# A Hymba layer on one core: the per-layer-embedding projection moved, operands and splits respread, two gate products reordered

## The chip, the cores and the metric

The kernel runs on one core of a Trainium2 chip. The metric is the device time of one execution in microseconds (us), taken as the median of several runs. Beside it stands one profiled execution, from which all rows below come.

## The reference, cut to what matters

One decoder layer for 512 positions of width 2048, in float32. The change touches what stands behind the mixers:

```
h = h + concat([oa, ob, oc]) @ w_out                  # 2048 x 2048
c = rmsnorm(h, ffn_norm)
hg = causal_conv3(c @ w_gate) + conv_b                # 2048 x 5632
h = h + (gelu(hg) * (c @ w_up)) @ w_down              # 5632 x 2048
e = rmsnorm(h, ple_norm)
h = h + sigmoid(e @ w_ple_gate) * (p @ w_ple_proj)    # 2048 x 2048 and 256 x 2048
```

## The kernel before, in words

**Split products.** Each float32 operand is split in two float32r parts, high and low, and a product is three matmuls: high x high, high x low, low x high. A weight chunk is split by a cast on ScalarE (L163, tile `wh`) and a subtraction on VectorE (L164, `wl`).

**Stages on TensorE, in order of time:** the input projection and the mixers, to about 785 us; `w_out`, four column blocks, the last one in two halves, to about 900; `w_gate` and `w_up` as Strassen-Winograd products of 2x2 blocks (classes Pair and Product, seven products P1 to P7 a pair) to about 1793; `w_down` in three passes over 44 row tiles, the first for column blocks 0 and 1 in eight PSUM banks, the second for block 2 and the third for block 3 in four; `w_ple_gate` as Winograd products by halves (classes Columns and Half, `run_half` L450, column blocks c = 0 to 3) from about 2314 to 2488; then the tail of the last output tiles. The projection of p by `w_ple_proj`, 16 banks of six matmuls, is spliced into the second pass of `w_down`; its results go to DRAM (`ppd`) and come back as `pp` when a gate block is finished (`finish_ple`, L521).

**What sets the order.** Everything is issued in program order, and each engine takes its instructions in that order. Side work is written as Python generators in the list `bg`; `tick()` (L129), called at fixed places between matmul groups, takes one step of each. So a `yield` more in a generator moves all that follows it by one tick. `later` holds evictions that are issued after the next product or half. `advance_split(upto)` (L341) issues the two split instructions of the weight chunks up to a number, and whatever combination of blocks on VectorE they need (L251, L254, L306 to L312); the number says how far ahead of their use chunks are split. DMAs are issued on SyncE's queue (SP), in program order too; one that writes a buffer still in use holds up those behind it.

**Buffers.** 69 pages of 128x512 float32 (`page`, L94) serve nearly everything: residual tiles `h`, normalised sums, `hid`, `ppe`, `ps`, `pu`. Of weight chunks there are 4 high and 4 low buffers and 3 raw ones. PSUM has 4 `g` and 4 `m` banks; `x` of a gate block is a `g` bank, `y` and `z` are `m` banks.

**Steps that the change touches.** `operands` (L1245): transposes of h on TensorE (L1264) into an `m` bank, copies to SBUF on ScalarE with the norm's gain (L1266), then sums on VectorE (L1282) and splits (ScalarE L1294, VectorE L1299). `evac_o2` (L1209) adds a `w_out` bank to the residual (L1212), `evac_down` (L1455) a `w_down` bank (L1458). `stat` (L647) sums squares on ScalarE (L649), `finish` (L651) makes 1/rms of them on GpSimd (L118 to L122), `broadcast` (L658) spreads it over the partitions by matmuls (L667). `hid_split` (L1409) loads a tile of the hidden layer and splits it (L1415, L1417). `load_p` (L1481) loads p and transposes it (L1492). `evac_half` (L485) copies `x` to SBUF (L488) and adds halves (L495).

Of the kernel before, what the change touches and what calls it, by code (L numbers as in the profile page):

```python
# [52 lines left out]
def hybrid_layer_kernel(  # L53
# [343 lines left out]
    def run_product(c, ks):  # L397
# [3 lines left out]
        advance_split(products[0, "P1"].i + 4 if ks[-1] < 7 else c.i + 3)  # L401
# [48 lines left out]
    def run_half(c):  # L450
# [17 lines left out]
        for k in range(4):  # L468
            ah, al = eop[OPERAND[kind], 4 * h + k]
            for t in range(2):  # L470
                o, a = ps[:, t * 256 : t * 256 + 256], slice(t * P, t * P + P)
                f = st and h == 0 and k == 0 and t == 0
                skip = t == 1 or not st
                PE.matmul(o, ah[:, a], vh[:, k, :], start=f, stop=False, skip_group_check=skip)  # L474
                PE.matmul(o, ah[:, a], vl[:, k, :], start=False, stop=False, skip_group_check=skip)
                PE.matmul(o, al[:, a], vh[:, k, :], start=False, stop=h == 1 and k == 3, skip_group_check=skip)
            if k == 1:
                tick()
        while later:
            later.pop(0)()  # L480
# [4 lines left out]
    def evac_half(g, kind):  # L485
        if kind in ("P1", "P6", "P7"):
            g.s[kind] = page("ps")
            ACT.copy(g.s[kind], g.x)  # L488
        if kind in ("P2", "P7", "P3"):
            q, a, th, s = dict(P2=(g.__dict__.get("y"), "P1", 0, 0), P7=(g.z, "P7", 1, 1), P3=(g.z, "P6", 0, 1))[kind]  # L490
            u = page("pu")
            if kind == "P3" and g.c == 3:
                for i in range(2):
                    v = slice(i * 256, i * 256 + 256)
                    DVE.tensor_tensor(u[:, v], q[:, v], g.s[a][:, v], op=ALU.add)  # L495
                    for _ in finish_ple(g, u, th, s, u, [i]):
                        pass
                return
# [9 lines left out]
    def run_groups(on_start=None):  # L508
# [20 lines left out]
        splice(flat)  # L529
# [87 lines left out]
    class Act:  # L617
# [615 lines left out]
    def stats_store(c):  # L1233
        while state["operands"] < 2 * c + 1:
            yield
        for t in range(NT):
# [3 lines left out]
            yield  # L1240
        if c == 3:
# [3 lines left out]
    def operands(kps, gain, dst):  # L1245

        m, n = T // 2, len(kps)
        if n > 1 and dst is eop and kps[0] == 6:
            at = [[page("at").rearrange("p (i t) -> p i t", i=2) for _ in range(2)] for _ in range(2)]
        else:  # L1250
            if n > 1:
                at = [xtile("T").rearrange("p (i t) -> p i t", i=2) for _ in range(2)]
            elif kps[0] == 6:
                t = xtile("T").rearrange("p (r i t) -> p r i t", r=2, i=1)
                at = [t[:, r, :, :] for r in range(2)]
            else:
                at = [page("at").rearrange("p (i t) -> p i t", i=1) for _ in range(2)]
            at = [[t[:, :, :m], t[:, :, m:]] for t in at]
        for k in range(2 * n):
# [11 lines left out]
        (a11, a21), (a12, a22) = at  # L1271

        while n == 1 and kps[0] == 6 and "mixed" not in state:
            yield
        temps = []
        if n == 1 and kps[0] == 6:
# [25 lines left out]

        p1 = high("A11", a11)
        s1 = temp(a21, a22, ALU.add)
        p5 = high("S1", s1)
        low(*p1)
        s2 = temp(s1, a11, ALU.subtract)
        p2 = high("A12", a12)
        low(*p5)
        low(*p2)  # L1310
# [462 lines left out]
```

## Time and profile before

| | us |
|---|---|
| median of 3 runs | 2497.28 (2496.26 to 2498.15) |
| profiled execution | 2497.11 |
| its span, first to last instruction | 2495.4 |
| TensorE busy in the span | 2464.0 |
| VectorE busy | 1534.4 |
| ScalarE busy | 1065.4 |

TensorE is busy nearly all the time, so the interest lies in the stretches where it is not, and in those where its clock fell from 2.4 to 1.2 GHz. A view by windows gives for each stretch the busy time of each engine, the share of full clock that was granted, and the DMA share; the view of waits names who ended TensorE's idle times; the timeline of an engine then shows what stood in its queue.

### The profile page before, as it was taken

How to read it: one execution, taken by the hardware profiler on the slowest of the kernel's cores; microseconds unless marked ns; L12 is line 12 of the kernel's file. 1: busy time of each engine (PE TensorE's matmuls, PEld its weight loads, DVE VectorE, ACT ScalarE, POOL GpSimd, SP SyncE). 2: the span in 40 equal slices, each digit the busy share in tenths (PEclk: the TensorE clock that was granted, in tenths of full speed). 3: DMA queues.
4: the chain of work that ended last, by engine and by line, in shares of the span. 5: the costliest groups of instructions: out<-in, count | busy, mean ns of one | idle time of the engine just before them, and what ended most of it. 6: DMA issues, size and time to landing. Idle time of an engine off the chain costs nothing.

```text
span 2495.4 us, 38383 instructions
## 1 busy us (share of the span) xinstructions
PE 2464.0 (99%) x15628; PEld 2225.0 (89%) x15628; DVE 1534.4 (61%) x2021; ACT 1065.4 (43%) x1612; POOL 140.1 (6%) x232
## 2 busy tenths in 40 slices
PE   9999999999999999999999999999999999999898
PEld 7888898888888889999999999999988877878898
DVE  5253535545465578888878888888633355354787
ACT  5222234444442454444444444444432254253544
POOL 1232400201000000000000000000000000000100
PEclk9999999999999999999999999999999999999999
DMA  5322222233233333434434343434444457666455
GB/s 178 102 68 85 69 85 81 81 93 93 84 108 113 119 120 110 127 115 122 120 110 128 110 129 108 127 115 123 148 142 145 143 189 238 198 222 205 126 186 186
DMA packets 324635, 321.45 MB, mean 129 GB/s; under 512 B 13691, under 2 KB 243812, under 8 KB 324458
## 3 DMA queue, kind: packets, MB, share of 16 engines
q1 hardware_dynamic: 324426, 319.00, 42.0%
q8 instruction: 122, 2.00, 0.3%
q14 instruction: 55, 0.45, 0.1%
q10 hardware_dynamic: 32, 0.01, 0.0%
HBM read 290.63 MB, written 28.32 MB: 128 GB/s over the span
## 4 chain that ended last, share of the span: by engine, by line
PE 95%; DVE 2%; DMA 1%; ACT 1%; issue 0%; POOL 0%; SPq 0%; ACTq 0%; DVEq 0%
PE g L388 13%; PE g L386 13%; PE g L387 13%; PE x L420 7%; PE x L418 7%; PE x L419 7%; PE m L420 5%; PE m L418 5%; PE m L419 5%; PE m L388 2%; PE m L387 2%; PE m L386 2%; PE g L379 1%; PE g L381 1%; PE g L380 1%; PE x L474 1%
## 5 line engine op out<-in xcount | busy, mean ns | idle before, releaser
L164 DVE TENSOR_TENSOR wl<-raw,wh 128x1024 fp32r<-128x1024 f32 (+1 forms) x334 | 411.2, 1232 | 403.2 <-ACT wh L163 401.9
L163 ACT CAST wh<-raw 128x1024 fp32r<-128x1024 f32 (+1 forms) x334 | 347.0, 1042 | 339.3 <-PE g L388 250.7
L418 PE MATMUL x<-sh,wh 128*128 128x256 f32 x1408 | 397.5, 282 | 0.1
L420 PE MATMUL x<-sh,wl 128*128 128x256 f32 x1408 | 397.3, 282 | 0.0
L419 PE MATMUL x<-sl,wh 128*128 128x256 f32 x1408 | 396.9, 282 | 0.0
L164 DVE TENSOR_TENSOR wl<-T,wh 128x1024 fp32r<-128x1024 f32 x208 | 254.4, 1223 | 133.9 <-ACT wh L163 132.8
L420 PE MATMUL m<-sh,wl 128*128 128x256 f32 x1056 | 298.7, 283 | 0.0
L418 PE MATMUL m<-sh,wh 128*128 128x256 f32 x1056 | 298.7, 283 | 0.0
L419 PE MATMUL m<-sl,wh 128*128 128x256 f32 x1056 | 298.4, 283 | 0.0
L386 PE MATMUL g<-wh,ah 128*128 128x512 f32 (+2 forms) x768 | 297.0, 387 | 1.2 <-ACT ah L641 1.2
L388 PE MATMUL g<-wh,al 128*128 128x512 f32 (+2 forms) x768 | 289.2, 377 | 0.0
L387 PE MATMUL g<-wl,ah 128*128 128x512 f32 (+2 forms) x768 | 288.0, 375 | 0.0
L418 PEld LDWEIGHTS x<-sh,wh 128*128 128x128 f32 x1408 | 267.5, 190 | 0.3 <-ACT ps L435 0.3
L419 PEld LDWEIGHTS x<-sl,wh 128*128 128x128 f32 x1408 | 267.5, 190 | 0.0
L420 PEld LDWEIGHTS x<-sh,wl 128*128 128x128 f32 x1408 | 267.4, 190 | 0.0
L163 ACT CAST wh<-T 128x1024 fp32r<-128x1024 f32 x208 | 217.9, 1048 | 111.5 <-PE m L419 29.3
L386 PE MATMUL g<-wh,hh 128*128 128x512 f32 x528 | 208.5, 395 | 1.0 <-ACT hh L1415 1.0
L388 PE MATMUL g<-wh,hl 128*128 128x512 f32 x528 | 208.3, 395 | 0.5 <-DVE hl L1417 0.5
L387 PE MATMUL g<-wl,hh 128*128 128x512 f32 x528 | 208.0, 394 | 0.0
L418 PEld LDWEIGHTS m<-sh,wh 128*128 128x128 f32 x1056 | 201.4, 191 | 0.0
L420 PEld LDWEIGHTS m<-sh,wl 128*128 128x128 f32 x1056 | 201.3, 191 | 0.0
L419 PEld LDWEIGHTS m<-sl,wh 128*128 128x128 f32 x1056 | 201.3, 191 | 0.0
(297 smaller groups left out, 4504.4 us busy)
## 6 DMA issues: line engine op xcount, KB each, us to landing
raw<-in_w_down_dram SPq DMA_DIRECT2D x88, 512.0 KB, 5.2
raw<-in_w_in_dram SPq DMA_DIRECT2D x82, 512.0 KB, 3.7
raw<-in_w_gate_dram SPq DMA_DIRECT2D x66, 512.0 KB, 3.8
raw<-in_w_up_dram SPq DMA_DIRECT2D x66, 512.0 KB, 3.8
hid<-hid SPq DMA_DIRECT2D x132, 256.0 KB, 6.1
raw<-in_w_out_dram SPq DMA_DIRECT2D x32, 512.0 KB, 3.8
b<-in_w_gate_dram SPq DMA_DIRECT2D x22, 512.0 KB, 7.1
b<-in_w_up_dram SPq DMA_DIRECT2D x22, 512.0 KB
```

The source lines that it names most:

```text
L163: ACT.copy(c.h_, src)
L164: DVE.tensor_tensor(c.l_, src, c.h_.bitcast(F32), op=ALU.subtract)
L379: PE.matmul(ps, wh, ah, start=st, stop=False)
L380: PE.matmul(ps, wh, al, start=False, stop=False)
L381: PE.matmul(ps, wl, ah, start=False, stop=sp)
L386: PE.matmul(o, th, ch, start=st, stop=False)
L387: PE.matmul(o, th, cl, start=False, stop=False)
L388: PE.matmul(o, tl, ch, start=False, stop=sp)
L418: PE.matmul(ps, vh[:, k, :], ah, start=st and k == 0, stop=False, skip_group_check=not st)
L419: PE.matmul(ps, vh[:, k, :], al, start=False, stop=False, skip_group_check=not st)
L420: PE.matmul(ps, vl[:, k, :], ah, start=False, stop=k == 7, skip_group_check=not st)
L474: PE.matmul(o, ah[:, a], vh[:, k, :], start=f, stop=False, skip_group_check=skip)
```

## The change

It consists of these parts.

1. **w_out to w_gate.** Chunks of the first product pair are split 2, 3 or 4 chunks ahead (by product P1, P5, P2), where it was 4 for all. The sums of squares of the third and fourth column block come on every second tick, the third's three ticks later. The broadcast of 1/rms waits one tick more, and a Gelu of one column is issued ahead of it.
2. **Operands.** A transposed bank is copied in one ScalarE instruction of 512 columns, where it was two of 256. In those for the gate (`dst is eop`) the sums and splits are spread over more ticks, and each of blocks 0 to 2 starts 12 ticks later; block 3's are made in two pieces.
3. **w_down.** The hidden tiles of each pass have a dictionary of their own, and the next pass's first tiles are loaded and split before the pass that runs has ended; residual tiles are loaded earlier. p is transposed four ticks later.
4. **Projection.** Block 0's four banks are placed between the second and the third pass, those of blocks 1 to 3 between the third pass and the gate, in `g` banks. All sixteen banks are copied out by ScalarE; it was eight by ScalarE and eight by VectorE. At these pass changes chunks are split further ahead (`nxt`).
5. **Gate.** In block 0, P3 comes ahead of P2's second half and of P4, and P5's sum is copied to SBUF. In block 3, P4's halves stand around P3, and its last half runs by row tiles, each finished as it is done; P3 is finished in the usual way.

```diff
-        advance_split(products[0, "P1"].i + 4 if ks[-1] < 7 else c.i + 3)
+        advance_split(products[0, "P1"].i + dict(P1=2, P5=3, P2=4)[kind] if ks[-1] < 7 else c.i + 3)
...
-        for k in range(4):
+        end = (g.c, kind, h) == (3, "P4", 1)
+        for k, t in [(k, t) for t in range(2) for k in range(4)] if end else [(k, t) for k in range(4) for t in range(2)]:
...
+            if end and k == 3:
+                while later:
+                    later.pop(0)()
+                for _ in finish_ple(g, page("pu"), 1, 0, g.x, [t]):
+                    pass
+        if end:
+            return
...
-        if kind in ("P1", "P6", "P7"):
+        if kind in ("P1", "P6", "P7") or kind == "P5" and g.c == 0:
             g.s[kind] = page("ps")
-            ACT.copy(g.s[kind], g.x)
+            ACT.copy(g.s[kind], g.z if kind == "P5" else g.x)
         if kind in ("P2", "P7", "P3"):
-            q, a, th, s = dict(P2=(g.__dict__.get("y"), "P1", 0, 0), P7=(g.z, "P7", 1, 1), P3=(g.z, "P6", 0, 1))[kind]
+            q, a, th, s = dict(P2=(g.__dict__.get("y"), "P1", 0, 0), P7=(g.s.get("P5", g.z), "P7", 1, 1), P3=(g.z, "P6", 0, 1))[kind]
             u = page("pu")
...
-            if kind == "P3" and g.c == 3:
-                for i in range(2):
-                    v = slice(i * 256, i * 256 + 256)
-                    DVE.tensor_tensor(u[:, v], q[:, v], g.s[a][:, v], op=ALU.add)
-                    for _ in finish_ple(g, u, th, s, u, [i]):
-                        pass
-                return
...
-        splice(flat)
...
+            if isinstance(g, Group) and (g.w is w_ple_proj or nxt and (nxt[0].early or nxt[0].look > 3 or nxt[0].g.w is w_ple_proj)):
+                nxt = [c for f in flat[n + 1 : n + 4] for c in f[3]][: 2 if g.w is w_out else 4 - len(cs)]
...
+            if self is cT:
+                ACT.activation(warm, neghalf[:, 0:1], AF.Gelu_apprx_tanh)
...
-            yield
-            yield
+            for _ in range(2 if self is aT else 3):
+                yield
...
+        for _ in range(3 if c == 2 else 0):
+            yield
...
+            if c > 1:
+                yield
...
-            for j in range(2):
-                ACT.activation(
-                    at[k % 2][j][:, k // 2, :], ps[:, j * m : j * m + m], AF.Copy, scale=gain[:, kt : kt + 1]
-                )
+            ACT.activation(at[k % 2][:, k // 2, :], ps, AF.Copy, scale=gain[:, kt : kt + 1])
...
+        pause = [None] * (dst is eop)
         p1 = high("A11", a11)
         s1 = temp(a21, a22, ALU.add)
         p5 = high("S1", s1)
         low(*p1)
...
-    def hid_split(kt):
+    def hid_split(n, kt):
...
-        hid[kt] = hh, hl
-
-    def split_all(wide):
+        hids[n][kt] = hh, hl
+
+    def split_all(n):
+
         for kt in range(NC):
-            while kt > cur["kt"] + (5 if wide else 9) or kt not in hdd:
-                yield
-            bg.append(hid_split(kt))
-            for _ in range(3 if wide else kt % 2):
+            while kt > curs[n] + (9 if n else 5) or kt not in hdd:
+                yield
+            bg.append(hid_split(n, kt))
+            for _ in range(kt % 2 if n else 3):
...
+        for _ in range(12 if c == 3 else 0):
+            yield
...
-            yield from operands((2 * c, 2 * c + 1), g_ple, eop)
+            for _ in range(12 if c < 3 else 0):
+                yield
+            for kps in [(2 * c, 2 * c + 1)] if c < 3 else [(6,), (7,)]:
+                for step in operands(kps, g_ple, eop):
+                    for _ in range(2 if c < 3 else 1):
...
-            if b % 2 == 0:
-                ACT.copy(t, ps)
-            else:
-                DVE.tensor_copy(t, ps)
+            ACT.copy(t, ps)
...
+    def proj(c, banks):
+
+        def need(kts):
+            while pl[1] is None:
+                tick()
+        return Group(
+            2, w_ple_proj, krow, [(c * NB, NB)], lambda kt: (ph[kt], pl[kt]), [0, 1], evac_pp(c), need=need, banks=banks
+        )
+
...
-            if NC - 8 < kts[0] <= NC - 4 and kts[0] % 4 == 0:
+            if kts[0] == (24 if n else NC - 4):
                 bg.append(load_h2(cs))
-            need_hidden(kts)
+            if n < 2 and kts[0] == NC - 4 * (n + 1):
+                bg.append(split_all(n + 1))
+            need_hidden(n, kts)
...
-        second = groups[-1]
+        if cs[0] == 3:
+            groups.append(proj(0, "mmmm"))
...
-    def splice(flat):
-
-        at = [n for n, (g, i, kts, cs) in enumerate(flat) if g is second]
-        for c in (3, 2, 1, 0):
-            g = proj[c]
-            flat.insert(at[2 * c + 4], (g, 0, [0, 1], [Chunk(g, [0, 1])]))
+    for c in (1, 2, 3):
+        groups.append(proj(c, "gggg"))
...
-        order += [(c, "P4", 0), (c, "P4", 1), (c, "P3", 0), (c, "P3", 1)]
+        order += {
+            0: [(0, "P3", 0), (0, "P3", 1), (0, "P2", 1), (0, "P4", 0), (0, "P4", 1)],
+            3: [(3, "P4", 0), (3, "P3", 0), (3, "P3", 1), (3, "P4", 1)],
+        }.get(c) or [(c, k, h) for k in ("P4", "P3") for h in range(2)]
...
```

VectorE where w_out ends and the first gate product begins, before. `h<-g` is the residual's sum (L1212), `wl` a split, `T<-b` a combination of weight blocks, `sl` and `st` are operands:

```order
L1299 TENSOR_TENSOR sl_7572<-b_1376_7528,sh_7568 128x256
L1212 TENSOR_TENSOR h_6505<-g_7469,h_6505 128x256
L1212 TENSOR_TENSOR h_6537<-g_7482,h_6537 128x256
L164 TENSOR_TENSOR wl_7601<-T_7508,wh_7600 128x1024
L251 TENSOR_TENSOR T_7606<-b_1375_7514,T_7508 128x1024
L164 TENSOR_TENSOR wl_7609<-raw_7438,wh_7608 128x1024
L254 TENSOR_TENSOR T_7612<-b_1375_7514,raw_7364 128x1024
L164 TENSOR_TENSOR wl_7615<-T_7606,wh_7614 128x1024
L1212 TENSOR_TENSOR h_6558<-g_7495,h_6558 128x256
L1282 TENSOR_TENSOR st_7658<-at_7641,at_7642 128x256
L1299 TENSOR_TENSOR sl_7534<-at_7641,sh_7529 128x256
```

Five instructions of 1024 columns stand ahead of the last `h<-g` (L1212). The same place in the changed kernel, where L1215 is the residual's sum, L1283 and L1300 are the operands' and L1269 has taken L1266's place:

```order
L1215 TENSOR_TENSOR h_6505<-g_7443,h_6505 128x256
L1215 TENSOR_TENSOR h_6537<-g_7460,h_6537 128x256
L1215 TENSOR_TENSOR h_6558<-g_7473,h_6558 128x256
L1283 TENSOR_TENSOR st_7630<-at_7615,at_7616 128x256
L1300 TENSOR_TENSOR sl_7516<-at_7615,sh_7511 128x256
L1283 TENSOR_TENSOR st_7634<-st_7630,at_7615 128x256
L1300 TENSOR_TENSOR sl_7521<-st_7630,sh_7514 128x256
L1300 TENSOR_TENSOR sl_7523<-at_7616,sh_7519 128x256
L251 TENSOR_TENSOR T_7639<-b_1372_7496,T_7490 128x1024
L164 TENSOR_TENSOR wl_7642<-raw_7414,wh_7641 128x1024
L1283 TENSOR_TENSOR st_7659<-at_7615 128x256
```

The last `h<-g` now stands ahead of the combinations and splits, which follow the operands.

VectorE at the end of w_down's second pass, before (L1458 adds a bank to the residual, L1417 splits a hidden tile):

```order
L1458 SCALAR_TENSOR_TENSOR h_20821<-g_19601,rstd_97,h_20821 128x512
L1458 SCALAR_TENSOR_TENSOR h_20842<-g_19647,rstd_97,h_20842 128x512
L1458 SCALAR_TENSOR_TENSOR h_20857<-g_19683,rstd_97,h_20857 128x512
L1417 TENSOR_TENSOR hl_20891<-hid_20874,hh_20890 128x512
L1417 TENSOR_TENSOR hl_20894<-hid_20876,hh_20893 128x512
L1417 TENSOR_TENSOR hl_20901<-hid_20878,hh_20900 128x512
L1417 TENSOR_TENSOR hl_20904<-hid_20880,hh_20903 128x512
L164 TENSOR_TENSOR wl_20915<-raw_20764,wh_20914 128x1024
L1458 SCALAR_TENSOR_TENSOR h_20872<-g_19719,rstd_97,h_20872 128x512
```

The fourth sum stands behind four hidden splits and a weight split. In the changed kernel (L1468, L1423):

```order
L1300 TENSOR_TENSOR sl_20568<-T_20455,sh_20562 128x512
L164 TENSOR_TENSOR wl_20571<-raw_20441,wh_20570 128x1024
L1468 SCALAR_TENSOR_TENSOR h_20182<-g_19562,rstd_97,h_20182 128x512
L1468 SCALAR_TENSOR_TENSOR h_20207<-g_19582,rstd_97,h_20207 128x512
L1283 TENSOR_TENSOR st_20608<-st_20564,T_20455 128x512
L1300 TENSOR_TENSOR sl_20612<-st_20564,sh_20566 128x512
L1423 TENSOR_TENSOR hl_20590<-hid_20491,hh_20589 128x512
L1423 TENSOR_TENSOR hl_20593<-hid_20493,hh_20592 128x512
L1468 SCALAR_TENSOR_TENSOR h_20232<-g_19599,rstd_97,h_20232 128x512
L1423 TENSOR_TENSOR hl_20617<-hid_20526,hh_20616 128x512
L1423 TENSOR_TENSOR hl_20620<-hid_20528,hh_20619 128x512
L1468 SCALAR_TENSOR_TENSOR h_20257<-g_19616,rstd_97,h_20257 128x512
```

Two hidden splits in place of four, and operands of an earlier block, stand between the sums; the matmuls of the projection's first block lie beside them on TensorE.

ScalarE ahead of the gate's first products, before (L649 is a sum of squares, L488 the copy of `x`):

```order
L1294 CAST sh_22045<-at_21934 128x512
L1294 CAST sh_22047<-st_22041 128x512
L649 ACTIVATE junk_22053,ss_98<-h_21890 128x512
L163 CAST wh_22085<-T_21693 128x1024
L163 CAST wh_22114<-T_21829 128x1024
L488 COPY ps_22142<-x_21905 128x512
L163 CAST wh_22145<-raw_21775 128x1024
L163 CAST wh_22181<-raw_21831 128x1024
L163 CAST wh_22216<-raw_22149 128x1024
L488 COPY ps_22220<-x_21905 128x512
```

Four weight casts stand around the copy of `x`, and the projection's copies are far ahead of this place. In the changed kernel, in the projection of blocks 2 and 3, with the semaphores that a row waits for (those of DMAs are called DMAHW; L1518 copies a projection bank to SBUF):

```order
L1518 COPY ppe_21860<-g_21829 128x512 [waits DMAHW5_49,PE_49]
L1269 ACTIVATE at_21864<-m_21866,gains 128x512 [waits DVE_49,PE_49]
L1269 ACTIVATE at_21865<-m_21872,gains 128x512 [waits DMAHW6_49,PE_49]
L1295 CAST sh_21741<-at_21864 128x256 [waits Activation_49]
L1295 CAST sh_21745<-st_21879 128x256 [waits DVE_49]
L1518 COPY ppe_21890<-g_21853 128x512 [waits DMAHW0_49]
L1295 CAST sh_21768<-at_21865 128x256 [waits Activation_49]
L1518 COPY ppe_21905<-g_21883 128x512 [waits DMAHW7_49,DVE_49,PE_49]
L1518 COPY ppe_21917<-g_21898 128x512 [waits DMAHW3_49,PE_49,Activation_49]
L1295 CAST sh_21804<-st_21894 128x256
L1295 CAST sh_21808<-st_21922 128x256 [waits DVE_49]
L163 CAST wh_21926<-T_21660 128x1024
```

Twelve such copies and the second piece of block 3's operands stand in this queue now; all four of the copies shown wait for a DMA, three of them for TensorE as well; so does the second `at` row.

## Rows read from the trace of the kernel before

**Rows 1.** The page's head: span, and busy time of each engine with its share and count.

```profile
span 2495.4 us, 38383 instructions
PE 2464.0 (99%) x15628; PEld 2225.0 (89%) x15628; DVE 1534.4 (61%) x2021; ACT 1065.4 (43%) x1612; POOL 140.1 (6%) x232
```

**Rows 2.** Windows: from and to, length, busy time and count of each engine, then the granted clock (1.00 is full), the DMA share and GB/s.

```profile
870.00:890.00 20.00, 17.92 (x145) 17.24 (x145) 12.37 (x21) 12.42 (x28) 0.00 (x0) 1.00 0.27 84
900.00:920.00 20.00, 15.87 (x117) 15.26 (x117) 14.49 (x26) 12.06 (x26) 4.52 (x6) 0.91 0.33 97
2050.00:2065.00 15.00, 13.57 (x67) 10.30 (x65) 12.55 (x19) 12.97 (x25) 0.00 (x0) 1.00 0.70 240
2070.00:2184.00 114.00, 114.00 (x497) 92.94 (x496) 48.23 (x60) 39.88 (x55) 0.00 (x0) 1.00 0.66 216
2184.00:2200.00 16.00, 12.46 (x54) 9.47 (x53) 9.70 (x14) 10.83 (x21) 0.00 (x0) 0.89 0.51 188
2200.00:2312.00 112.00, 112.00 (x488) 91.20 (x487) 52.48 (x69) 45.35 (x69) 0.00 (x0) 1.00 0.66 213
2316.00:2332.00 16.00, 14.47 (x120) 14.07 (x119) 11.07 (x15) 10.53 (x23) 0.00 (x0) 1.00 0.05 17
2332.00:2350.00 18.00, 11.68 (x73) 11.27 (x72) 14.08 (x15) 7.83 (x11) 9.62 (x6) 0.81 0.29 87
2350.00:2484.00 134.00, 134.00 (x1126) 134.00 (x1125) 106.17 (x109) 65.95 (x86) 0.00 (x0) 1.00 0.66 208
```

**Rows 3.** Waits of TensorE over the whole span: line waited at, what ended the wait, us in total, times, longest.

```profile
PE x L474 <- ACT ps L488: 6.3, 2, 3.4
PE m L1264 <- DVE h L1212: 3.3, 2, 2.3
PE m L1264 <- DVE h L1458: 2.5, 1, 2.5
PE m L667 <- DVE dg L662: 1.8, 1, 1.8
```

**Rows 4.** Timeline at the end of w_out, VectorE and then TensorE: start, us, engine, line, operation and tiles, and in brackets the idle time before it with what ended it.

```profile
898.47 1.22 DVE L164 TENSOR_TENSOR wl<-T,wh 128x1024 fp32r<-128x1024 f32 x1
...
903.01 1.22 DVE L164 TENSOR_TENSOR wl<-T,wh 128x1024 fp32r<-128x1024 f32 x1
904.14 0.42 DVE L1212 TENSOR_TENSOR h<-g,h 128x256 f32<-128x256 f32 x1
...
904.62 0.77 PE L1264 MATMUL m<-ident,h 128*128 128x128 f32 x5 [2.26 <-DVE h L1212]
```

**Rows 5.** Timeline of GpSimd in the first gate products: the first and the last of six instructions.

```profile
912.57 0.20 POOL L654 TENSOR_SCALAR a<-a 128x4 f32<-128x4 f32 x1 [106.22 <-DVE a L653]
...
917.30 0.20 POOL L122 TENSOR_TENSOR rstd<-rstd,nt 128x4 f32<-128x4 f32 x1
```

**Rows 6.** Timeline between w_down's second and third pass, VectorE and then TensorE.

```profile
2186.30 2.63 DVE L1417 TENSOR_TENSOR hl<-hid,hh 128x512 fp32r<-128x512 f32 x4 [1.06 <-ACT hh L1415]
2190.53 1.22 DVE L164 TENSOR_TENSOR wl<-raw,wh 128x1024 fp32r<-128x1024 f32 x1 [1.59 <-ACT wh L163]
2191.67 0.74 DVE L1458 SCALAR_TENSOR_TENSOR h<-g,rstd,h 128x512 f32<-128x512 f32 x1
...
2192.47 1.25 PE L1264 MATMUL m<-ident,h 128*128 128x128 f32 x5 [2.50 <-DVE h L1458]
```

**Rows 7.** Timeline at the start of the gate, ScalarE and then SyncE's queue.

```profile
2334.63 1.05 ACT L163 CAST wh<-T 128x1024 fp32r<-128x1024 f32 x1 [0.90 <-DVE T L308]
2335.58 0.58 ACT L488 COPY ps<-x 128x512 f32<-128x512 f32 x1
...
2344.86 1.04 ACT L163 CAST wh<-raw 128x1024 fp32r<-128x1024 f32 x1 [4.62 <-DMA raw<-in_w_ple_gate_dram]
2345.82 0.58 ACT L488 COPY ps<-x 128x512 f32<-128x512 f32 x1
...
2340.25 0.38 SPq L286 DMA_DIRECT2D raw<-in_w_ple_gate_dram  x1
```

**Rows 8.** Timeline of the tail, VectorE and then SyncE's queue.

```profile
2488.44 0.42 DVE L495 TENSOR_TENSOR pu<-m,ps 128x256 f32<-128x256 f32 x1 [3.43 <-PE m L476]
...
2491.69 0.42 DVE L1532 TENSOR_TENSOR pu<-pu,pp 128x256 f32<-128x256 f32 x1
...
2485.08 7.44 SPq L1536 DMA_DIRECT2D out_dram<-pu  x4
```

**Rows 9.** DMA issues over the whole span: tiles, queue, count, KB each, median us from issue to landing.

```profile
hid<-hid SPq DMA_DIRECT2D x132, 256.0 KB, 6.1
x<-in_x_dram SPq DMA_DIRECT2D x16, 256.0 KB, 7.6
ppd<-ppe SPq DMA_DIRECT2D x16, 256.0 KB, 3.4
```

**Rows 10.** Groups of ScalarE instructions by line and form: count, busy us, mean ns of one, idle time before them.

```profile
L1266 ACT ACTIVATE T<-m,gains 128x256 f32<-128x256 f32 x52 | 20.5, 474 | 22.9 <-PE m L1264 22.8
L649 ACT ACTIVATE junk<-h 128x512 f32<-128x512 f32 x32 | 20.2, 631 | 3.0 <-DVE h L1458 3.0
L641 ACT ACTIVATE ah<-m,g_attn 128x512 fp32r<-128x512 f32 x16 | 11.0, 687 | 16.4 <-PE m L638 16.4
L1504 ACT COPY ppe<-m 128x512 f32<-128x512 f32 x8 | 4.7, 588 | 10.9 <-PE m L388 10.9
```

More of the change, by code (lines that the diff above doesn't have):

```diff
@@ L467, in run_half @@
         vl = c.l_.rearrange("p (k n) -> p k n", k=4)
-        for k in range(4):
+        end = (g.c, kind, h) == (3, "P4", 1)
+        for k, t in [(k, t) for t in range(2) for k in range(4)] if end else [(k, t) for k in range(4) for t in range(2)]:
             ah, al = eop[OPERAND[kind], 4 * h + k]
[L470 to L477, printed above, removed]
-                tick()
+            o, a = ps[:, t * 256 : t * 256 + 256], slice(t * P, t * P + P)
+            f = st and h == 0 and k == 0 and t == 0
+            skip = t == 1 or not st
+            PE.matmul(o, ah[:, a], vh[:, k, :], start=f, stop=False, skip_group_check=skip)
+            PE.matmul(o, ah[:, a], vl[:, k, :], start=False, stop=False, skip_group_check=skip)
+            PE.matmul(o, al[:, a], vh[:, k, :], start=False, stop=h == 1 and k == 3, skip_group_check=skip)
+            if (k, t) == (1, 1):
+                tick()
+            if end and k == 3:
[5 more added lines that the diff above has]
+            return
         while later:
@@ L1247, in operands @@
         m, n = T // 2, len(kps)
-        if n > 1 and dst is eop and kps[0] == 6:
-            at = [[page("at").rearrange("p (i t) -> p i t", i=2) for _ in range(2)] for _ in range(2)]
-        else:
[L1251 to L1255, printed above, removed]
-            else:
-                at = [page("at").rearrange("p (i t) -> p i t", i=1) for _ in range(2)]
-            at = [[t[:, :, :m], t[:, :, m:]] for t in at]
+        scarce = n == 1 and kps[0] == 6 and dst is sop
+        if n > 1:
+            at = [xtile("T").rearrange("p (i t) -> p i t", i=2) for _ in range(2)]
+        elif scarce:
+            t = xtile("T").rearrange("p (r i t) -> p r i t", r=2, i=1)
+            at = [t[:, r, :, :] for r in range(2)]
+        else:
+            at = [page("at").rearrange("p (i t) -> p i t", i=1) for _ in range(2)]
         for k in range(2 * n):
@@ L1264, in operands @@
                 PE.transpose(ps[:, t * P : t * P + P], hp[t][c][:, o : o + P], ident)
-            for j in range(2):
-                ACT.activation(
-                    at[k % 2][j][:, k // 2, :], ps[:, j * m : j * m + m], AF.Copy, scale=gain[:, kt : kt + 1]
-                )
+            ACT.activation(at[k % 2][:, k // 2, :], ps, AF.Copy, scale=gain[:, kt : kt + 1])
             if k % 2 and n > 1:
                 yield
-        (a11, a21), (a12, a22) = at
-        while n == 1 and kps[0] == 6 and "mixed" not in state:
+        (a11, a21), (a12, a22) = [(t[:, :, :m], t[:, :, m:]) for t in at]
+        while scarce and "mixed" not in state:
             yield
         temps = []
-        if n == 1 and kps[0] == 6:
+        if scarce:
             t = xtile("b22").rearrange("p (k i t) -> p k i t", k=4, i=1)
@@ L1306, in operands @@
         low(*p1)
+        yield from pause
         s2 = temp(s1, a11, ALU.subtract)
@@ L1309, in operands @@
         low(*p5)
+        yield from pause
         low(*p2)
@@ L1315, in operands @@
         low(*p6)
+        yield from pause
         s4 = temp(a12, s2, ALU.subtract)
@@ L1318, in operands @@
         p4 = high("A22", a22)
+        yield from pause
         p3 = high("S4", s4)
@@ L1355, in hybrid_layer_kernel @@
     NC = D_FF // P
-    cur = {}
+    curs = [-6] * 3
     gates = {}
@@ L1433, in load_h2, with need_hidden @@
                 yield
-    def need_hidden(kts):
-        while kts[-1] not in hid:
+    def need_hidden(n, kts):
+        curs[n] = max(curs[n], -1)
+        while kts[-1] not in hids[n]:
             assert bg
             tick()
-        cur["kt"] = kts[-1]
+        curs[n] = kts[-1]
     hd2 = {}
@@ L1485, in load_p @@
             SP.dma_start(pt[t // 2][:, (t % 2) * PLE : (t % 2) * PLE + PLE], p[t * P : t * P + P, :])
-        yield
-        yield
+        for _ in range(6):
+            yield
         for k in range(2):
@@ L1655, in hybrid_layer_kernel @@
         two = len(cs) > 1
-        second = groups[-1]
+        if cs[0] == 3:
+            groups.append(proj(0, "mmmm"))
         groups.append(
-            Group(2, w_down, krow, [(cs[0] * NB, len(cs) * NB)], hid.__getitem__, list(range(NC)), evac_down(cs),
+            Group(2, w_down, krow, [(cs[0] * NB, len(cs) * NB)], hids[n].__getitem__, list(range(NC)), evac_down(cs),
                   need=need, kpg=2 if two else 4, kpc=1 if two else 2, banks="mmmmgggg" if two else "gggg")
         )
-    proj = [
-        Group(2, w_ple_proj, krow, [(c * NB, NB)], lambda kt: (ph[kt], pl[kt]), [0, 1], evac_pp(c), banks="mmmm")
-        for c in range(4)
-    ]
```

22 lines of the change are left out of this document (9 added, 13 removed).

## The prediction

> **What bounds the kernel now.** First the page's head [rows 1]: TensorE is busy 2464.0 of 2495.4 us, VectorE 61%, ScalarE 43%. The change adds and removes no matmul, it only moves some, so what it can win is the 31.4 us in which TensorE stands, and the time that it loses at the lower clock. Then the windows, which show where both lie [rows 2]. In a window, length less busy time is the idle time, and length times (1 less granted clock) is what the fall from 2.4 to 1.2 GHz costs. 900 to 920: 4.13 idle, 20 x 0.09 = 1.8 of clock. 870 to 890: 2.08 idle. 2050 to 2065: 1.43. 2184 to 2200: 3.54 and 16 x 0.11 = 1.76. 2316 to 2350: 1.53 + 6.32 = 7.85 and 18 x 0.19 = 3.42. Together 26.0 us. The long stretches between them, 2070 to 2184, 2200 to 2312 and 2350 to 2484, have no idle time and full clock: nothing can be won in them, only lost. Of the other idle time the start of the kernel holds most, which the change leaves alone, and the tail behind the last matmul about 7 us. Last the waits [rows 3], which name the releasers: the copy of x to SBUF (6.3 us in two), the sums into h (3.3 and 2.5), the norm's diagonal (1.8). None is a shortage of an engine over a stage; each is a short instruction that stands in a queue behind longer ones.
>
> **A. w_out to the first gate product: gain 1.7 us, between -1.8 and 6.** The last sum into h starts at 904.14, straight behind VectorE work that runs without a hole from 898.47, five instructions of 1.14 us from start to start, 5.7 us [rows 4]; the transposes wait 2.26 us for it. The changed order has that sum ahead of all five, so this wait goes, and with it the 1.8 of clock that followed it. The third block's sums of squares, four of 0.63 [rows 10], move behind the weight cast they had delayed; of the 2.08 us of the window before, I take 0.9 to stay, since its first wait hangs on a bank's sum behind a weight split, and that order is unchanged. What is late next: the five instructions prepare the products that follow, and they now come after the operands. Upper bound of that wait is all five, 5.7; the lower is nothing; I take two of them late, 2 x 1.14 = 2.3, at P2, as three have P5's matmuls to hide them, one more (1.2) at P6 behind sums of squares on ScalarE, and 0.25 at P7. GpSimd's chain for the norm lasts from 912.57 to 917.50 [rows 5] and is not shortened; its wait of 1.8 at the broadcast moves and stays as about 1.65. Sum: 2.08 + 4.13 + 1.8 = 8.0, less 0.9, 1.65 and 3.75, is 1.7.
>
> **B. First to second pass of w_down: gain 1.0 us, between -1.6 and 1.4.** The 1.43 us are three short waits, at p's transposes and at one hidden split. Waiting four ticks more before the transposes, and having the next pass's first four hidden tiles ready, removes them. But hidden tiles 4 to 7 stand on SP behind a weight load that writes a raw buffer still being split. A hidden load lands 6.1 us after issue [rows 9]; by the order they would land up to 3 us late, or in time. I take 0.4 of that.
>
> **C. Second to third pass: gain 5.0 us, between 2 and 5.3.** Here the sum at 2191.67 stood behind four hidden splits and a weight split (from 2186.30), and the transposes waited 2.50 us [rows 6]; the clock fell behind that. In the changed order two hidden splits lie between the sums, the hidden tiles are loaded ahead, and 5.5 us of matmuls (block 0's projection: 24 of 0.2295 us, from 112.00 us for 488 [rows 2]) lie on TensorE while VectorE clears the four banks. Its work there, four sums, four hidden splits, two operand instructions and a weight split, is 4 x 0.75 + 4 x 0.65 + 2 x 0.6 + 1.14 = 7.9 us, but the third pass needs its banks one after the other, 2.8 us apart, so the last is needed 8.3 us after the projection. I leave 0.3 us for small waits. **The second pass without the projection** is denser in transfers, but it becomes what the third already is, which moved 213 GB/s with a full TensorE [rows 2]: nothing lost there. The projection's 96 matmuls cost 22.0 us wherever they stand.
>
> **D. Third pass to the gate: gain 9.3 us, between 5 and 11.27.** Before, the copy of x waited in ScalarE's queue behind a cast (2334.63) that waited for VectorE, 3.4 us for TensorE, and the second time behind a cast (2344.86) that had waited 4.62 us for a load issued at 2340.25, 2.9 us [rows 3, 7]; the clock fell after each. With 16.5 us of projection (72 matmuls) in front, the loads and splits of the gate have that much more time, and both waits lose their cause. So do the two at 2328 to 2330 (1.53). Against this, ScalarE gets twelve copies of 0.59 [rows 10], 7.1 us, eight of them its own before, but not here; four operand copies of 0.69 in place of 0.47 a half, 2.7; some fourteen casts of 0.36, 5.0; six weight casts of 1.05, 6.3: 21 us of work. TensorE has 16.5 of projection, 1.75 of transposes and three half products of 24 x 0.119 (134.00 us for 1126, [rows 2]) = 8.6, 26.8 us, before the first copy of x is needed. It fits, with a fifth to spare. The copies also need pages: in the order, several wait for a DMA, the landing of an earlier copy's write to DRAM, 3.4 us after issue [rows 9]. By the order and these durations I put one such write at 15.05 us after the pass ends; 15.05 + 3.4 + 0.6 = 19.05 against 18.4, when TensorE wants that bank for x: 0.65, up to 2.4 if landings take 5. Another 0.7 at P7, since P6's copy is on the same bank, and 0.65 for whatever of P5's new copy (0.59) shows. New waits: 2.0; 11.27 less 2.0 is 9.3.
>
> Two rules of the Trainium skill price this otherwise. Its page DMA: Bandwidth & Descriptors (Anatomy of one DMA) puts a transfer (on GpSimd's path) at a fixed 2.0 us plus bytes over 436 GB/s, most of it the receipt of the write. For 256 KB that would be an estimated 2.6 us, and the wait of 0.65 would not arise (2478.9 in place of 2479.5); the row has 3.4, and I keep it. Its page TensorE: Matmul & The Clock Gate (Part 4: PE-mode transpose) says that transposes do not count as TensorE activity as matmuls do, and this speaks against transposes next to the new waits. In the row at 904.62 five transposes do stand between the wait and the fall of the clock, but at 885 to 890 two waits of about 1 us around eight transposes left the clock at 1.00 [rows 2, 4]; by the rule, a wait at P1 behind block 3's transposes would bring one more fall, some 1.7 us, and 2481.2.
>
> **E. Tail: gain 0.75 us, between 0 and 2.** VectorE's chain after the last matmul lasts from 2488.44 to 2492.11, two rounds of sum, sigmoid, product, sum; then the last of four output writes lands [rows 8]. Now the last half's first tile is finished while the second is multiplied. Behind the last matmul stand a sigmoid, a product and a sum of 0.42 each, then P3's two sigmoids and two instructions of 0.69: about 2.9 us.
>
> **Sum.** 1.7 + 1.0 + 5.0 + 9.3 + 0.75 = 17.75 us. The profiled execution took 2497.11, 0.17 less than the median; 2497.28 - 17.75 = 2479.5.
>
> **Rivals.**
>
> *Waits replaced.* The places change, the waits remain. At A all five preparations come late (3.4 more than taken) and the clock falls (1.8); at D landings of 5 us and a cast behind a late load give 6 in place of 2, with one fall (1.7). That takes 5.2 + 5.7 = 10.9 back: 2490.4. For it: every wait of before is of this kind, and the new orders put the same long instructions behind other short ones. Against it: in D a fifth of ScalarE's time is free.
>
> *Nearly all goes.* The new waits hide: 8.0 + 1.4 + 5.3 + 11.27 + 2.0 = 28 us, 2469.3. For it: the waits I add are each within about 2 us of nothing. Against it: GpSimd's chain cannot shrink, so 2471 is more likely than 2469.
>
> *Slower: a chain of pages.* In D six instructions of ScalarE wait for landed writes. If each in turn waits for one, they take 6 x (L + 0.6) for a landing time L, against 26.8 us that hide them. At 3.4 that is 24 us and nothing shows. The writes share the DMA engines with the gate's loads, and the slowest row of its size is 7.6 [rows 9]. At 8 us, 51.6 - 26.8 = 24.8 us appear: 2504.3. It decides from where it eats 22.5 us, L = 7.6. Against it: the DMA share is 0.05 at 2316 to 2332 [rows 2], so the queue is nearly empty there.
>
> *It does not do what it says.* Splits and loads may be held by buffers, not by the ticks, so that the respread orders wait as before and only the projection's move counts; with P6's wait left, gains and new waits would cancel, about 2495.
>
> **How the numbers follow.** The forecast (2475 to 2485) gets 0.56, waits replaced (2485 to 2494) 0.20, nearly all gone (2468 to 2475) 0.15, the chain of pages 0.05, no effect 0.04. The likeliest time is 2479.5. A range from 2469 to 2491 leaves out the last two and part of the second. About 0.2%, 5 us, is what a measurement can tell here: faster than 2492.3 has 0.56 + 0.15 + 0.17 = 0.88, within 0.2% 0.03 + 0.04 = 0.07, slower 0.05.
>
> **What would show it right or wrong.** In the changed kernel's trace: no wait at the transposes behind w_out, and a new one of 2 to 3 us before P2; the 1.65 at the broadcast; full clock from 2180 to 2360, and no wait over 1 us at the third pass; at the gate's start, waits under 1 us at P1 and P7, in place of 3.4 and 2.9. Wrong would be: clock below 1.00 where I have short waits, ScalarE waiting for DMA in the projection for more than 20 us, a wait of 2 us or more at the second pass's second group.

## The result and the profile after

| | before | after |
|---|---|---|
| median, 6 runs each (us) | 2496.82 (2496.26 to 2498.15) | 2479.43 (2478.01 to 2484.94) |
| ratio of the two | | 0.9934, 95% interval 0.9921 to 0.9947 |
| profiled execution, span (us) | 2497.11, 2495.4 | 2478.01, 2476.3 |

The forecast was 2479.5. The head of the page after: span, then busy time of each engine [rows 1].

```profile
span 2476.3 us, 38365 instructions
PE 2457.5 (99%) x15628; PEld 2218.6 (90%) x15628; DVE 1529.9 (62%) x2023; ACT 1063.3 (43%) x1597; POOL 133.9 (5%) x232
```

The windows after, with the columns of [rows 2]; from the second pass change on, the same work stands earlier.

```profile
870.00:890.00 20.00, 19.26 (x161) 18.80 (x161) 12.38 (x20) 12.48 (x23) 0.00 (x0) 1.00 0.31 91
900.00:920.00 20.00, 17.25 (x137) 16.34 (x136) 15.24 (x26) 14.30 (x28) 2.01 (x6) 1.00 0.33 93
2030.00:2050.00 20.00, 19.52 (x87) 15.30 (x85) 10.15 (x13) 7.87 (x12) 0.00 (x0) 1.00 0.69 225
2158.00:2184.00 26.00, 26.00 (x113) 20.69 (x112) 15.21 (x20) 16.10 (x30) 0.00 (x0) 1.00 0.69 224
2285.00:2310.00 25.00, 22.56 (x115) 18.18 (x114) 13.71 (x26) 16.39 (x33) 0.00 (x0) 1.00 0.57 181
2310.00:2330.00 20.00, 19.32 (x162) 19.12 (x161) 14.97 (x15) 12.65 (x21) 0.00 (x0) 1.00 0.49 161
```

The clock is full in all of them. By the prediction's own measure (idle time plus what the clock costs), against [rows 2]:

| place | before | after | gain | forecast |
|---|---|---|---|---|
| A, w_out to first product | 8.0 | 0.74 + 2.75 = 3.5 | 4.5 | 1.7 |
| B, first to second pass | 1.43 | 0.48 | 1.0 | 1.0 |
| C, second to third pass | 5.3 | 0 | 5.3 | 5.0 |
| D, third pass to gate | 11.27 | 2.44 + 0.68 = 3.1 | 8.2 | 9.3 |

At the tail, TensorE's end to the last write took 7.0 us [rows 8] and takes 6.1, less a new wait of 0.6: 0.3. The five make 19.3, and the two spans differ by 19.1; the median moved by 17.4, since the changed kernel's profiled execution was the fastest of its six. The waits of TensorE after at the places of the change, as in [rows 3]:

```profile
PE g L386 <- ACT ppe L1518: 2.3, 2, 1.7
PE m L420 <- DVE wl L164: 1.4, 1, 1.4
PE g L386 <- DVE h L1215: 0.7, 1, 0.7
PE x L474 <- ACT ps L495: 0.7, 1, 0.7
PE x L418 <- ACT ps L435: 0.6, 1, 0.6
PE m L418 <- ACT wh L163: 0.6, 1, 0.6
PE x L474 <- ACT pu L1540: 0.6, 1, 0.6
```

No wait for the sums into h at the transposes is left, and none at the norm's broadcast. The longest of them is new: it stands in the projection itself, at a copy of a projection bank (L1518). ScalarE's timeline there shows why, two waits for landed writes:

```profile
2299.36 0.59 ACT L1518 COPY ppe<-g 128x512 f32<-128x512 f32 x1 [2.08 <-DMA ppd<-ppe]
2299.84 0.70 ACT L1269 ACTIVATE at<-m,gains 128x512 f32<-128x512 f32 x1
2301.23 0.69 ACT L1269 ACTIVATE at<-m,gains 128x512 f32<-128x512 f32 x1 [0.69 <-DMA ppd<-ppe]
```

So the sum came out. The experiments ask whether its terms, and the reasons behind them, did.

### The profile page after: what moved, and what is told of

The parts are those of the page before. It is cut to its first block, busy times and chain, and to the rows that moved or that the text cites. A ratio compares the mean times of both kernels' runs of the same rounds, so it can differ in the third digit from the quotient of the medians.

```text
span 2476.3 us, 38365 instructions
## 1 busy us (share of the span) xinstructions
PE 2457.5 (99%) x15628; PEld 2218.6 (90%) x15628; DVE 1529.9 (62%) x2023; ACT 1063.3 (43%) x1597; POOL 133.9 (5%) x232
## 4 chain that ended last, share of the span: by engine, by line
PE 96%; DMA 2%; DVE 1%; ACT 1%; issue 0%; POOL 0%; SPq 0%; ACTq 0%; POOLq 0%; DVEq 0%
PE g L386 14%; PE g L388 14%; PE g L387 14%; PE x L418 7%; PE x L420 7%; PE x L419 7%; PE m L420 5%; PE m L418 5%; PE m L419 5%; PE m L388 2%; PE m L387 2%; PE m L386 2%; PE g L379 1%; PE g L381 1%; PE g L380 1%; PE m L797 1%
```

## The experiments

All kernels were timed against the kernel before, five rounds each. The theory on trial first is the prediction's: each place gains by itself, from the part of the change made there.

**1. The move alone**, on the kernel before:

```diff
-        splice(flat)
...
+        if cs[0] == 3:
+            groups.append(proj(0, "mmmm"))
...
+    for c in (1, 2, 3):
+        groups.append(proj(c, "gggg"))
```

> The kernel before with part 4 alone: the projection's block 0 between the second and third pass, blocks 1 to 3 in g banks ahead of the gate; copies by ScalarE and VectorE in turn as before, and all else as before. Sum theory (each place gains by itself): the gate's two waits for the copy of x (3.4 and 2.9) and the two falls of the clock behind them go, 9 to 11 us, some 2 us of new waits come, and at the second pass change the wait of 2.5 and its 1.8 of clock shrink as 5.5 us of matmuls cover the sums: together 10 to 14 us, 2483 to 2487, with the waits behind w_out (2.3, 1.8) unchanged. Rival (the respread operands and early hidden tiles are what makes the move pay): new waits in the projection eat most of it, 2490 or more.

Measured: 2502.47, ratio to before 1.0022 (1.0013 to 1.0032). It is slower than before. The first expectation is far off; the rival's "2490 or more" holds, but not by its waits in the projection, which are 3.7 us in all (2.7 below and one of 1.0): most of the time is lost at the third pass. The waits of TensorE:

```profile
PE g L386 <- ACT hh L1414: 9.1, 1, 9.1
PE x L474 <- ACT ps L488: 4.3, 1, 4.3
PE g L386 <- ACT ppe L1503: 2.7, 1, 2.7
```

The third pass waits 9.1 us for its first hidden tile, and SP's queue (start, time, tiles, count) tells why. A row's time includes what its DMAs waited for:

```profile
2161.06 7.48 SPq L186 DMA_DIRECT2D raw<-in_w_down_dram  x2
2168.59 3.83 SPq L1507 DMA_DIRECT2D ppd<-ppe  x3
2172.48 1.90 SPq L1449 DMA_DIRECT2D hd<-h  x4
2174.48 1.52 SPq L1410 DMA_DIRECT2D hid<-hid  x2
```

The loads `hid<-hid` stand behind weight loads, the projection's writes and the residual's, and the clock falls to 0.69 behind the wait (2176 to 2190). And at the gate one of the two waits for the copy of x is still there, behind a cast that waits for a load, as in [rows 7], although 16.5 us of matmuls now stand in front.

**2. Split distance back to 4** in the changed kernel:

```diff
-        advance_split(products[0, "P1"].i + dict(P1=2, P5=3, P2=4)[kind] if ks[-1] < 7 else c.i + 3)
+        advance_split(products[0, "P1"].i + 4 if ks[-1] < 7 else c.i + 3)
```

> The changed kernel with its split-ahead distance set back to 4 for P1, P5 and P2. Sum theory: the last sum into h stands behind five long VectorE instructions again, the transposes wait about 2.3 us and the clock falls behind it (1.8), while the waits of 0.6 and 1.4 ahead of P2's first products go: 1.5 to 3 us slower than the changed kernel, 2481 to 2483. Rival (the sums of squares on every second tick are what frees this place): no wait at the transposes, and within 1 us of the changed kernel.

Measured: 2479.24 (0.9934, 0.9920 to 0.9947), the changed kernel's own time. TensorE's waits do what the theory said, one of 2.8 us at the transposes in place of 0.6, 1.4 and 0.6:

```profile
PE m L1268 <- DVE h L1215: 2.8, 1, 2.8
```

but the window with this wait (it ends at 903.72) and with what follows it has the full clock (columns as above):

```profile
900.00:920.00 20.00, 16.98 (x139) 16.34 (x139) 13.38 (x26) 13.62 (x27) 2.01 (x6) 1.00 0.36 105
```

A wait was exchanged for others of about the same sum.

**3. No early load of hidden tiles** in the changed kernel:

```diff
+                if n:
+                    curs[n] = -1
+                    bg.append(split_all(n))
...
-            if n < 2 and kts[0] == NC - 4 * (n + 1):
-                bg.append(split_all(n + 1))
```

> The changed kernel with each pass's hidden tiles loaded and split only from the pass's own start, as before. Sum theory: waits of 1 to 3 us for hidden tiles at both pass changes, VectorE's sums behind hidden splits again: 3 to 5 us slower, 2482 to 2485. Rival (the projection's 5.5 us of matmuls between the passes cover the loads by themselves): nothing at the second pass change, at most 1.5 us at the first, 2479 to 2481.

Measured: 2492.17 (0.9984, 0.9975 to 0.9992), 12.7 us over the changed kernel; both expectations were far too low. A wait of TensorE:

```profile
PE g L386 <- ACT hh L1421: 9.6, 1, 9.6
```

SP's queue ahead of it:

```profile
2162.02 0.95 SPq L1520 DMA_DIRECT2D ppd<-ppe  x2
2163.02 7.71 SPq L1417 DMA_DIRECT2D hid<-hid  x9
```

and the window around both:

```profile
2158.00:2176.00 18.00, 7.14 (x23) 4.95 (x22) 11.10 (x17) 11.14 (x20) 0.00 (x0) 0.73 0.69 243
```

The same wait as in experiment 1: the nine loads go out behind the projection's writes, and the clock in this window is 0.73.

**4. The old order of the gate's block 0** in the changed kernel:

```diff
-        if kind in ("P1", "P6", "P7") or kind == "P5" and g.c == 0:
+        if kind in ("P1", "P6", "P7"):
...
-            0: [(0, "P3", 0), (0, "P3", 1), (0, "P2", 1), (0, "P4", 0), (0, "P4", 1)],
...
```

> The changed kernel with block 0 of the gate in the old order (P2's second half ahead of P4, P4 ahead of P3, P5's sum left in its bank); the projection stays ahead of the gate. Sum theory: the projection's 16.5 us is what removed the waits at the gate's start, so the order is worth 0 to 1 us: 2479 to 2481, no wait over 1 us at P1 and P7. Rival (the order frees the bank and the loads that P6 and P7 wait for): a wait of 2 to 3 us at P7 or behind it returns, perhaps with a fall of the clock, 2482 to 2485.

Measured: 2481.38 (0.9940, 0.9927 to 0.9952), 2.0 us over the changed kernel, whose own runs scatter more than that, so the trace has to decide. VectorE, ScalarE, SP, and last what that load waited for:

```profile
2322.46 2.50 DVE L164 TENSOR_TENSOR wl<-raw,wh 128x1024 fp32r<-128x1024 f32 x2
...
2328.40 1.04 ACT L163 CAST wh<-raw 128x1024 fp32r<-128x1024 f32 x1 [3.46 <-DMA raw<-in_w_ple_gate_dram]
2329.35 0.58 ACT L495 COPY ps<-x 128x512 f32<-128x512 f32 x1
...
2323.71 0.38 SPq L286 DMA_DIRECT2D raw<-in_w_ple_gate_dram  x1
...
SPq L286 <- DVE wl L164: 12.4, 1, 12.4
```

It is [rows 7] again. The load goes out at 2323.71, when the first of the two splits that VectorE starts at 2322.46 is over: it waited 12.4 us for that split, which frees a raw buffer. Its own cast waits 3.46 for it, and the copy of x behind the cast holds TensorE for 2.5. The theory's reason (16.5 us in front remove the cause) falls. In the changed kernel the load goes out no earlier:

```profile
2323.55 0.38 SPq L286 DMA_DIRECT2D raw<-in_w_ple_gate_dram  x1
```

There its cast is not due before 2331.18, since the new order puts products in front that do not need it.

After these four a second theory: the parts are conditions of each other. The move leaves a stretch in which SP holds the hidden loads; the early load closes it.

**5 and 6. Early load with the move, and alone**, on the kernel before (the dictionaries, `split_all(n + 1)` and the lines of experiment 3, reversed):

> The kernel before with the projection's move and the early load of the next pass's hidden tiles, and nothing else. Theory of the pair (the move leaves a stretch in which SP's queue holds the hidden loads behind the projection's writes; the early load alone closes it): the wait of 9.1 us for a hidden tile at the third pass goes, with the fall of the clock behind it, 11 to 13 us off the 2502.5 of the move alone: 2489 to 2492; at the gate 4.3 us of waits for the copy of x and 3.7 for the projection's copies stay. Rival (the places simply add up): 2497 less 5.5 at the pass change, 6.7 at the gate and 1.6 at the first change, 2482 to 2485.

> The kernel before with the early load of hidden tiles alone; the projection stays in the second pass. Theory of the pair: without the move there is little to close, only the waits of 1.0 for a hidden tile and part of the 2.5 and 1.8 behind the hidden splits: 1 to 5 us faster than before, 2492 to 2496. Rival (early loads are what the 12.7 us of the third experiment measured, whatever else stands): 2484 to 2487.

Measured: 2510.75 (1.0057, 1.0045 to 1.0070) and 2506.23 (1.0035, 1.0022 to 1.0047). Both are slower than before and than the move alone; all four expected times were wrong. In 5 the third pass now starts without a wait, but TensorE stands at its fifth hidden tile, after 48 matmuls on the four that were loaded early:

```profile
2199.82 0.79 PE L386 MATMUL g<-wh,hh 128*128 128x512 f32 x1 [8.72 <-ACT hh L1414]
...
2192.06 7.39 SPq L1410 DMA_DIRECT2D hid<-hid  x9
```

The next nine loads stand on SP behind weight loads, the projection's last write and the residual's: the wait of experiment 1 has moved, not gone. ScalarE, VectorE and SP of the early load alone (6), in the first pass change:

```profile
2038.04 1.57 ACT L1266 ACTIVATE T<-m,gains 128x256 f32<-128x256 f32 x4 [2.19 <-PE m L1264]
2039.48 1.06 ACT L163 CAST wh<-raw 128x1024 fp32r<-128x1024 f32 x1
...
2049.28 3.04 ACT L1266 ACTIVATE T<-m,gains 128x256 f32<-128x256 f32 x8
2052.18 1.17 ACT L1415 CAST hh<-hid 128x512 fp32r<-128x512 f32 x2
...
2040.58 1.23 DVE L164 TENSOR_TENSOR wl<-raw,wh 128x1024 fp32r<-128x1024 f32 x1 [3.43 <-ACT wh L163]
...
2028.93 13.27 SPq L186 DMA_DIRECT2D raw<-in_w_down_dram  x4
2042.25 4.52 SPq L1411 DMA_DIRECT2D hid<-hid  x8
```

The weight cast at 2039.48 stands behind an operand copy, VectorE's split at 2040.58 waits for the cast, the last of the four weight loads on SP waits for the raw buffer that the split frees, and behind that load stand the eight hidden loads, issued from 2042.25 on. ScalarE then makes operands and sums of squares up to the first hidden cast at 2052.18. This suggests a third condition: the operands must be out of ScalarE's way.

**7. No further look ahead** (the `nxt` lines removed) and **8. operands not spread** in the changed kernel:

```diff
-        pause = [None] * (dst is eop)
+        pause = []
...
-            for _ in range(12 if c < 3 else 0):
-                yield
...
```

> The changed kernel without the further look ahead for splits at pass changes. If the splits at the changes hide anyway: within 1 us of the changed kernel, 2479 to 2480.5. If they don't: a cast and a split, 1.05 and 1.22 us and a start of 1 us each, come late at up to five changes (two around the projection's first block, three ahead of the gate): 4 to 8 us slower, 2483 to 2487, with new waits for wh and wl.

> The changed kernel with the gate's operands made in one go again, without the 12 ticks and the steps between, and with the third block's last sums of squares not delayed. If the spread counts: seven casts of 0.6 and seven VectorE sums of 0.69 stand together ahead of hidden splits and of projection copies, waits of 1 to 3 us at two pass changes and in the projection: 2482 to 2486. If the move alone gives them cover: within 1 us, 2478.5 to 2480.5.

Measured: 2477.87 (0.9926, 0.9913 to 0.9938) and 2500.28 (1.0017, 1.0008 to 1.0026). The look ahead is worth nothing that can be measured; the spread is worth 20.9 us, far over what I expected. In 8, ScalarE is taken mostly by operands and sums from 2041 to 2055, and the next weight cast comes at 2055.82. A hidden cast at 2046.41 waits for no load; it stands behind the operands, and TensorE waits 2.84 us for it. So here the operands hold the casts themselves. The cast, and TensorE's waits in 8:

```profile
2046.41 1.14 ACT L1421 CAST hh<-hid 128x512 fp32r<-128x512 f32 x2
...
PE g L386 <- ACT hh L1421: 7.1, 2, 4.3
PE g L388 <- DVE hl L1423: 5.9, 2, 4.0
```

and the window at its first pass change, where the clock fell too:

```profile
2030.00:2070.00 40.00, 31.23 (x139) 24.77 (x138) 25.06 (x38) 25.94 (x52) 0.00 (x0) 0.83 0.52 177
```

In 7 the waits for projection copies are gone, and the writes land sooner. DMA issues between 2286 and 2310, first of the changed kernel, then of 7 (median us to landing last):

```profile
ppd<-ppe SPq DMA_DIRECT2D x11, 256.0 KB, 7.6
```

```profile
ppd<-ppe SPq DMA_DIRECT2D x12, 256.0 KB, 4.1
```

**9 to 12. What holds the projection's copies, and the tail**, in the changed kernel: the look ahead only where a product or the gate is next (`nxt and nxt[0].early`), copies in turn by ScalarE and VectorE, `end = False`, and the first two together.

> The changed kernel with the further look ahead only where a product or the gate comes next, so that the gate's weight loads stand behind, not ahead of, the projection's writes on SP. If loads that share the DMA engines with the writes are why ScalarE waits for landings (7.6 us against 4.1 without the look ahead): no waits for the projection's copies, and no late split at P2, 2 to 3 us faster than the changed kernel, 2476 to 2477.5. If the pages alone set it: the same waits of 2 to 3 us, 2479 to 2480.

> The changed kernel with every second copy of a projection bank on VectorE, as before. If the waits in the projection come from landed writes and pages: a copy waits as long on either engine, but ScalarE's operand copies no longer stand behind it, 0 to 1.5 us faster, 2478 to 2479.5. If ScalarE's load sets them: they go, 2476 to 2477. If VectorE then holds up the sums of the gate: 1 to 2 us slower, 2481.

> The changed kernel without the special last half: P4's halves still stand around P3 in block 3, but the last one runs and is finished as all others are. By the prediction's term the special half is worth 0.75 us at most; in the changed kernel's trace TensorE waits 0.6 us between the two row tiles for the sigmoid that reads the same bank, which takes most of it: -0.3 to 0.7 us against the changed kernel, 2479 to 2480.2. If the finish of the last half in one piece is what it replaces: sigmoid, product and sum over 512 columns behind the last matmul, 1 to 2 us slower, 2480.5 to 2481.5.

> The late gate loads and the copies in turn together. If both act on the same waits: as the better of the two alone, 2476 to 2477.5. If they add: 1 us below that.

Measured: 2478.35 (0.9928, 0.9915 to 0.9940), 2481.70 (0.9942, 0.9928 to 0.9956), 2477.87 (0.9928, 0.9915 to 0.9940) and 2480.01 (0.9935, 0.9922 to 0.9947). In 9 one gate load stands ahead of the seventh write on SP, where the changed kernel has three; the writes land after 3.9 us (median) and TensorE waits for no projection copy. With 7 this points to the loads that share the DMA engines. The time shows less than the 2 to 3 us expected, since a hidden tile now comes 1.0 late at the third pass. In 10, whose profiled execution was the slowest of its five (2486.38), TensorE's wait for copies moves to VectorE's and grows to 4.5, and VectorE stands 4.27 for a landing: the landing sets it, not ScalarE's load. TensorE's waits for weight splits on VectorE grow too, to 3.8 in five from 0.3 in the changed kernel, so the copies also stand in the gate's way, close to the third expectation. In 12 the writes land after 3.2 and no copy is waited for, but splits on VectorE come late, 2.9 in five waits; nothing adds. 11 is no slower than the changed kernel: its special last half is worth nothing that can be measured. No version beats the changed kernel beyond its interval; 7, 9 and 11 equal it with less code or fewer waits.

## Why the prediction was right, point by point

The size was right, 17.75 us forecast and 17.4 measured. So was the method, idle time and clock by windows, less a bound for each new wait, as far as where the time lay. That the time came within 0.1 us is luck: A gained 2.8 more than forecast, D 1.1 less, and the changed kernel's six runs spread over 6.9. At A, C and D a reason of the prediction failed.

- **A.** The named cause, a sum behind five long instructions, is real, but removing it is worth nothing in the changed kernel: experiment 2 puts it back at the same time. The gain of 4.5 is 1.34 us at 870 to 890, the broadcast's 1.8 and 1.8 of clock that no longer falls (in experiment 2, with the wait back, it does not fall either, so what keeps it full is open); the wait of 2.26 went, and others of about that size came, 0.6 and 1.4 at P2 (2.3 forecast) and 0.6 at P6 (1.2). The step that failed is that GpSimd's chain "is not shortened": it lasted 2.43 us, not 4.93 (below). It now ends at 918.19 and the broadcast stands at 920.27, so nothing of the 1.65 is left; how much of that the shorter chain did, and how much the broadcast's extra tick, no run sets apart.
- **B and C.** Right in size. The step that failed is that C's terms stand by themselves: the sum, the early load and the 5.5 us of cover were each taken as a help. The runs show one chain: SP holds hidden loads behind a weight load, that waits for VectorE's split, the split for a cast, and the cast stands behind operands on ScalarE. In experiments 1, 3 and 5 the projection's writes stand in that queue too, and in 8 the operands stand ahead of the hidden casts themselves. I had seen its first half, at B, and priced it at 0.4. Take away the early load and 12.7 us come back, the spread and 20.9; the move alone costs 5.9.
- **D.** 8.2 for 9.3. "Both waits lose their cause" failed: experiments 1 and 4 have the projection in front and still wait 4.3 and 2.5, because the load waits for a buffer that VectorE's split frees, not for time. The first of the two waits of before went with the move alone (1); the second went only with the new order, which needs the load later. The landing was mis-sized, 3.4 taken and 7.6 measured with the gate's loads among the writes (3.9 and 4.1 in experiments 9 and 7, which move them back), so the wait stands in the projection (2.3) and not at P1; P7's 0.7 was right. The estimate of 2.6 by the Trainium skill's figure for GpSimd's path (DMA: Bandwidth & Descriptors, Anatomy of one DMA) is further off: the measurement decides. The Trainium skill's rule that transposes do not count as matmuls do (TensorE: Matmul & The Clock Gate, Part 4: PE-mode transpose) met no case here: no wait came at P1, and the clock is 1.00 in that window.
- **The rival of pages.** Its threshold, landings of 7.6, was met, and the price did not come: ScalarE waited 2.08 and 0.69, since the six waits do not follow one another as I had it.
- **E.** 0.3 for 0.75: TensorE's 0.6 between the row tiles ate the rest, and experiment 11 finds no gain at all.

What stays open: which of the remaining differences of the early load alone (hidden tiles, order of stores) make its two further waits of 2.3 and 2.5. The changed kernel without the move alone was not measured, so what the move adds on top of the other parts is not shown.

## What to carry to other kernels

When a queue is in order, a part of a change has no price of its own: follow the chain from the waiting engine through the DMA queue to the buffer and to the instruction that frees it, and ask which parts cut that chain; time the parts alone and left out before explaining a sum. Here work moved in front of a wait did not remove it where the wait was for a buffer and not for time. A landing time is read from a stretch with the same traffic, not from the whole run.

## What the runs showed of the hardware that was not expected

GpSimd's chain for the norm took 4.93 us before, 912.57 to 917.50 [rows 5]. Its third to fifth instruction before:

```profile
913.94 1.01 POOL L119 TENSOR_TENSOR nt<-rstd 128x4 f32<-128x4 f32 x1
915.02 1.06 POOL L120 TENSOR_TENSOR nt<-nt,a 128x4 f32<-128x4 f32 x1
916.17 1.04 POOL L121 TENSOR_SCALAR nt<-nt 128x4 f32<-128x4 f32 x1
```

After, the chain reads:

```profile
915.76 0.20 POOL L655 TENSOR_SCALAR a<-a 128x4 f32<-128x4 f32 x1 [110.57 <-DVE a L654]
...
917.13 0.20 POOL L119 TENSOR_TENSOR nt<-rstd 128x4 f32<-128x4 f32 x1
917.41 0.20 POOL L120 TENSOR_TENSOR nt<-nt,a 128x4 f32<-128x4 f32 x1
917.70 0.20 POOL L121 TENSOR_SCALAR nt<-nt 128x4 f32<-128x4 f32 x1
917.99 0.20 POOL L122 TENSOR_TENSOR rstd<-rstd,nt 128x4 f32<-128x4 f32 x1
```

The three instructions became 0.20 us each; the second, L118, took 1.01 both times. Before, VectorE ran combinations and splits of 1.22 us from 913.66 to 917.16 beside them; after, it is idle for 2.22 us up to 918.22. The Trainium skill has a rule that would do this (SBUF — State Buffer, Terms): VectorE and GpSimd share a pair of ports, held for a whole instruction, and the loser blocks. The rows agree with it; no run sets the overlap by itself.

After a wait of 2.26 us the clock fell in the kernel before, 0.91 in 900 to 920 [rows 2, 4]; after one of 2.8 us at the same place in experiment 2 it stayed at 1.00 (900 to 920). The length of the wait alone does not decide it; what TensorE did before differs (two waits near 1 us at 885 to 889 before, one of 0.7 there), but no run sets the two apart. The projection's writes of 256 KB landed after 3.9 (experiment 9), 4.1 (7) or 7.6 us (changed kernel) in the median, by where the gate's loads stood among them in the queue.
